# Adding expert results to a DRAM sum by whole rows, one add per block of tokens

## The chip, the cores and the metric

One core of one Trainium2 chip runs the kernel. The metric is the device time of one execution in microseconds (us); lower is better. Engines are called as in the profile: PE (TensorE, matrix products), PEld (its weight loads), DVE (VectorE), ACT (ScalarE), POOL (GpSimd), SP (SyncE, which here only issues DMAs).

## The reference

A decoder layer for one sequence of 1024 tokens of width 1024: two mixing branches, a projection, then a mixture of experts (MoE) that takes most of the time. What matters here is the MoE:

```python
top_val, top_idx = lax.top_k(logits, TOP_K)            # 4 of 32 experts a token
gate = jax.nn.softmax(top_val, axis=-1)
...
def expert_block(args):                                # a block of one expert's tokens
    xblk, e = args
    gu = xblk @ w_gu[e] + b_gu[e]                      # 1024 x 2048
    g, up = gu[:, :D_FF], gu[:, D_FF:]
    g = jnp.minimum(g, SWIGLU_LIMIT)
    up = jnp.clip(up, -SWIGLU_LIMIT, SWIGLU_LIMIT)
    act = (up + 1.0) * (g * jax.nn.sigmoid(SWIGLU_ALPHA * g))
    return act @ w_down[e] + b_down[e]                 # 1024 x 1024
...
out = jnp.zeros((N + 1, D_), f32).at[tok_buf].add(yb * w_buf[:, None])[:N]
```

Each token is in the list of four experts, so its output row is a sum of four expert results times their gates. A root-mean-square norm and a residual follow.

## The kernel before

Up to 570 us the kernel computes the mixing branches and the routing. From about 590 to 1980 us it runs the MoE. The experts are ordered by how many tokens they got, and each rank has a fixed capacity (`CAPS`, from 396 down to 36 token columns, 4648 in all). The 32 ranks go in eight groups of four (`GROUPS`), each of some 580 columns. For one group the kernel first does the gate and up products of all four experts, one half of the columns (c = 0, 1) after the other, then the down products, expert by expert, again in halves of 512 columns.

Weights come in chunks of 1 MiB on SP's queue (L1581) into six buffers `ST`. ACT makes a 16-bit high part of a chunk (L1585) and DVE the 16-bit rest (L1588), into seven buffers `WH`/`WL`; PE multiplies high by high and low activations (L1791, L1792) and rest by high ones (L1800). Twelve chunks make one expert's matrices, four of them the down matrix.

Results of a down product are scaled from PSUM into `yT`, transposed, in a region of 12.375 KB per partition; each half of an expert has its own piece, and a new piece waits for the transposes that read the piece it overwrites (L1839 to L1846). When one half of an expert is done, `out_jobs` (L1751) makes three jobs for each block of up to 128 tokens: four PE transposes into one of two PSUM banks `ot_` (L1759), an eviction by ACT or DVE that scales by the gate into one of three buffers `yt_r` of 128 x 512 (L1602 or L143 in the profile, tile A), and an indirect DMA on POOL (L1765) that adds the rows of 512 floats to one of two DRAM tensors `ff_d[c]`, at the rows that the token list names. Adds to the same `ff_d[c]` follow one another: each waits until the one before has landed. There are 51 blocks and so 102 adds. POOL's queue also issues the 51 gathers of token rows (L1726) for the next group.

The order on each engine is made beforehand: a planner (`Job`, `run_jobs`) goes through the jobs with estimated durations, due times and lags and writes each engine's instructions in the order in which it would start them. An add is planned with 1.7 us on POOL and 7.0 us more until it has landed. The engines then run their streams strictly in order; an instruction that waits holds up all behind it.

After the MoE, small loops for overflowing experts run zero times, and the sum is loaded from `ff_d` by eight DMAs (L1980) and normalised (L1988 and on); the results leave by SP.

Of the kernel before, what the change touches and what calls it, by code (L numbers as in the profile page):

```python
# [23 lines left out]
D = 1024  # L24
# [24 lines left out]
def hybrid_layer_kernel(ctx: ExitStack, tc: tile.TileContext, I, out):  # L49
# [777 lines left out]
    ff_d = [dr.tile([NR, D // 2], F32, name=f"ff_d{i}") for i in range(2)]  # L827
# [10 lines left out]
    for b in range(NR // 128):  # L838
        for q in range(2):
            P.dma_start(ff_d[q][128 * b:128 * b + 128], zt)  # L840
# [671 lines left out]

    SA = [slot(f"A{i}") for i in range(7)]
    ST = [carve(t_, 0, 4, 512) for t_ in SA[:-1]]
    WT.append(SA[-1])
    WH, WL = [], []
    for t_ in WT:
        WH.append(carve(t_, 0, 4, 256).bitcast(F16))
        WL.append(carve(t_, 4, 4, 256).bitcast(F16))
# [8 lines left out]
    X0, A0, Y0, XG0 = 0, XKB, 2 * XKB, 2 * XKB + 2 * CAPS[0] / 64  # L1528
    assert XG0 + 12 <= 64, XG0
# [6 lines left out]
    def acc_col():  # L1536
        n_acc[0] += 1
        return gacc[:, n_acc[0] - 1:n_acc[0]]
# [32 lines left out]
    def load_chunk(n):  # L1571
        if n >= len(chunks):
            i = n - len(chunks)
            if i < 4:
                SP.dma_start(HH[i], h_d[256 * i:256 * i + 256].rearrange("(b p) c -> p b c", p=128))
            else:
                SP.dma_start(GF, bass.AP(tensor=RW_d.tensor, offset=RW_d[1, 24].offset, ap=[[0, 128], [1, 1024]]))
        else:
            x, name, col, kh = chunks[n]
            load_expert(x)  # L1580
            SP.dma_start(ST[n % NST], I[name][0][ds(x.e, 1), 512 * kh:512 * kh + 512, col:col + 512]  # L1581
                         .rearrange("o (k p) c -> p (o k) c", p=128))
# [10 lines left out]
    n_mm, Y_KB = [0], 2 * CAPS[0] / 64  # L1593
# [76 lines left out]
    subs, phase = [], []  # L1670
    for gi, g in enumerate(GROUPS):
        phase.append((len(chunks), len(subs)))
        for c in range(2):
            for r in g:
                for q, kind in enumerate("gu"):
                    subs += [(kind, ex[r], c, js, len(chunks)) for js in (J4 if CAPS[r] <= 256 else J2)]
                    chunks += [(ex[r], "exp_w_gu", 1024 * q + 512 * c, kh) for kh in range(2)]
        phase.append((len(chunks), len(subs)))
        for r in g:
            for c in range(2):  # L1680
                subs += [("d", ex[r], c, js, len(chunks)) for js in (J4 if CAPS[r] <= 256 else J2)]
                chunks += [(ex[r], "exp_w_down", 512 * c, kh) for kh in range(2)]
    last_use, first_use = {}, {}
    for i, u in enumerate(subs):
        for kh in range(2):
            last_use[u[4] + kh] = i
            first_use.setdefault(u[4] + kh, 2 * i + kh)
# [61 lines left out]
    ot_free, yt_free, added, n_ot = [None] * 2, [None] * len(yt_r), [None] * 2, [0]  # L1749

    def out_jobs(x, c, b, yT, due, after):  # L1751
        cb = min(128, x.C - 128 * b)
        q, y = n_ot[0] % 2, n_ot[0] % len(yt_r)
        n_ot[0] += 1
        pt, yt = ot_[q], yt_r[y]

        def transpose(e):
            for k in range(4):
                PE.transpose(pt[0:cb, k], yT[:, k, 128 * b:128 * b + cb], ident)  # L1759
        t_ = Job({"PE": 0.46}, due, after + [ot_free[q]], transpose)  # L1760
        ot_free[q] = Job({"ACT": act_us(512, True), "DVE": dve_us(512)}, due + 2, [t_, yt_free[y]],
                         lambda e: scaled(e, yt[0:cb], pt[0:cb].rearrange("p a b -> p (a b)"),
                                          x.lt[0:cb, b, 1:2].bitcast(F32)))
# [11 lines left out]
    def sub_jobs(i, kind, x, c, js, n):  # L1775
        C, nj = x.C, len(js)
# [5 lines left out]
        us = nj * 4 * (max(C / 2400, 0.0225) + 0.0026)  # L1782
        needs = [bank_free[q] for q in bi] + (a_ready[x.r] if kind == "d" else x_ready[x.r])

        def highs(kh):
            def put(e):
                wh = WH[(n + kh) % NWS]
                for q, j in enumerate(js):
                    for k in range(4):
                        w_, f_ = wh[:, k, 128 * j:128 * j + 128], 4 * kh + k  # L1790
                        PE.matmul(pp[q], w_, mh[:, f_], start=(f_ == 0 and q % per == 0), stop=False, skip_group_check=True)  # L1791
                        PE.matmul(pp[q], w_, ml[:, f_], start=False, stop=False, skip_group_check=True)  # L1792
            return put

        def lows(kh):
            def put(e):
                wl = WL[(n + kh) % NWS]
                for q, j in enumerate(js):
                    for k in range(4):
                        PE.matmul(pp[q], wl[:, k, 128 * j:128 * j + 128], mh[:, 4 * kh + k], start=False,  # L1800
                                  stop=(kh == 1 and k == 3), skip_group_check=True)
            return put
        for kh in range(2):
            s_ = Job({"PE": 2 * us}, 2 * i + kh, [step[0], hi_[n + kh]] + (needs if kh == 0 else []), highs(kh))
            step[0] = Job({"PE": us}, 2 * i + kh, [s_, lo_[n + kh]], lows(kh))
            use[n + kh] = step[0]
        due, end = 2 * i + 4, step[0]
# [11 lines left out]
        elif kind == "u":  # L1819
            q, gs, gj = gs_of[x.r, js]  # L1820
            w = nj * C
# [5 lines left out]
            def clamp(e):  # L1827
                ts(u_t[:, 0:w], u_t[:, 0:w], 8.0, OP.min, -6.0, OP.max)
                stt(gs[:, 0:w], gs[:, 0:w], G_MAX, u_t[:, 0:w], OP.min, OP.mult)
            g3 = gs[:, 0:w].rearrange("p (j c) -> p j c", j=nj)  # L1830
            ev = Job({"ACT": act_us(w, True, nj), "DVE": dve_us(w, nj)}, due, [end, u_free[0]], linear)
            u_free[0] = Job({"DVE": dve_us(w, 2) + w / 1920}, due, [ev, gj], clamp)
            ah = Job({"ACT": act_us(w), "DVE": dve_us(w, 1, 1920)}, due + 2, [u_free[0]],
                     lambda e: scaled(e, x.ah[:, f0:f0 + nj], g3, XS))
            gs_free[q] = Job({"DVE": dve_us(w)}, due + 2, [ah],
                             lambda e: stt(x.al[:, f0:f0 + nj], g3, XS, x.ah[:, f0:f0 + nj], OP.mult, OP.subtract))
            a_ready.setdefault(x.r, []).append(gs_free[q])
        else:
            if js[0] == 0:  # L1839
                w = C / 64  # L1840
                at = y_at[0] if y_at[0] + w <= Y_KB else 0.0
                old = [o for o in y_used if o[0] < at + w and at < o[1]]
                for o in old:
                    y_used.remove(o)
                y_at[0] = at + w
                y_of[x.r] = (view(Y0 + at, 4, C), [t_ for o in old for t_ in o[2]], (at, at + w, []), [])  # L1846
            yT, wait, place, evs = y_of[x.r]

            def results(e):
                for k, j in enumerate(js):  # L1850
                    scaled(e, yT[:, j], pp[k], RS, x.bias[16 + f0 + k])
# [24 lines left out]
    for i, u in enumerate(subs):  # L1876
        while made < min(len(chunks) + 5, u[4] + 2):
            chunk_jobs(made)
            made += 1
        if i_ph % 2 and i_ph < len(phase) - 1 and phase[i_ph][1] == i:  # L1880
            todo = [(ex[r], b) for r in GROUPS[i_ph // 2 + 1] for b in range(NBS[r])]
            span_ = 2 * (phase[i_ph + 1][1] - i)
            for k, (x, b) in enumerate(todo):
                token_jobs(x, b, 2 * i + (span_ - 4) * k / len(todo), [ld[phase[i_ph - 1][0]], step[0]])
# [23 lines left out]
    zt = view(Y0, 512)  # L1908
    with tc.For_i(0, nzr, 1) as it:
        V.memset(zt, 0.0)  # L1910
        for q in range(2):
            SP.dma_start(ff_d[q][ds(it * 128, 128)], zt)
# [3 lines left out]
    def float_block(e, lt, bias):  # L1916
# [25 lines left out]
        for c in range(4):  # L1942
# [9 lines left out]
            if c % 2:  # L1952
                for k in range(4):
                    PE.transpose(ot_[0][:, k], yT[:, k], ident)
                scaled("ACT", yt_r[0], ot_[0].rearrange("p a b -> p (a b)"), lt[:, 0, 1:2].bitcast(F32))
                P.indirect_dma_start(out=ff_d[c // 2], in_=yt_r[0], in_offset=None, compute_op=OP.add,
                                     out_offset=bass.IndirectOffsetOnAxis(ap=lt[:, 0, 0:1], axis=0))
# [20 lines left out]
    for i in range(4):  # L1978
        for q in range(2):
            (SP, A)[q].dma_start(ft[i][:, :, 512 * q:512 * q + 512],  # L1980
                                 ff_d[q][256 * i:256 * i + 256].rearrange("(b p) c -> p b c", p=128))
# [37 lines left out]
```

## Time and profile before

| | us |
|---|---|
| median of 3 runs | 2026.05 (2025.1 to 2028.08) |
| profiled execution, its time | 2024.69 |
| profiled execution, its span | 2022.9 |
| mean granted clock of TensorE in it | 0.948 |

The time is that of an execution as the device gives it; the span is from the first to the last instruction in the trace, 1.8 us less. Busy times are of that one execution. A group's mean duration times its count gives busy time, not time on the path; what an engine waited for is read from the idle time ahead of an instruction. The granted clock is a share of 2.4 GHz: 1.00 is 2.4, 0.50 is 1.2.

### The profile page before, as it was taken

What the parts mean: (1) busy time and instruction counts of PE and PEld (TensorE: products, weight loads), DVE (VectorE), ACT (ScalarE), POOL (GpSimd) and SP (SyncE); (2) the same over time, 40 slices, a digit from 0 to 9 for tenths busy, and PEclk for the clock granted to TensorE, in tenths of its full rate; (3) what the DMA queues carried; (4) which work ended last, traced back from release to release, by engine and by line L of the source; (5) the groups of instructions that cost most, each with busy time, mean ns of one, the idle gap of its engine ahead of it and who ended that gap; (6) DMA issues with size and microseconds to landing.
All of it is one profiled execution on the core that took longest, in us unless ns stands there. A gap on an engine that the chain in (4) does not pass through costs nothing. (4 is left out here: it accounts for less than half of the span.)

```text
span 2022.9 us, 53263 instructions
## 1 busy us (share of the span) xinstructions
PE 1806.0 (89%) x22354; PEld 1614.5 (80%) x22354; DVE 1544.2 (76%) x2396; ACT 1199.1 (59%) x1682; POOL 526.5 (26%) x495
## 2 busy tenths in 40 slices
PE   8678699998968999998998899999899889999970
PEld 3566588787858999998998899767799789999870
DVE  5766537568767997995997799689799868869835
ACT  3524133544226876875776677577688667768641
POOL 4720012203543025015104402400330330160043
PEclk8889899999978999999999899999999989999985
DMA  9176465323359999999999899888999999999874
GB/s 310 39 193 132 137 196 161 126 70 131 115 172 326 363 322 353 379 351 307 323 329 358 278 351 341 279 323 301 299 367 365 301 296 330 327 318 350 306 192 175
DMA packets 296804, 540.82 MB, mean 267 GB/s; under 512 B 41234, under 2 KB 66032, under 8 KB 296528
## 3 DMA queue, kind: packets, MB, share of 16 engines
q1 hardware_dynamic: 259504, 469.51, 67.5%
q0 software_dynamic: 30384, 60.49, 11.8%
q10 hardware_dynamic: 6672, 7.38, 1.1%
q8 instruction: 177, 2.90, 0.6%
q14 instruction: 67, 0.55, 0.1%
HBM read 489.57 MB, written 45.61 MB: 265 GB/s over the span
## 5 line engine op out<-in xcount | busy, mean ns | idle before, releaser
L1765 POOL DMA_INDIRECT ff_d<-A,S x102 | 260.7, 2555 | 353.8 <-DVE A L143 141.2
L1588 DVE SCALAR_TENSOR_TENSOR B<-A,B 128x2048 f16<-128x2048 f32 x110 | 249.5, 2285 | 33.1 <-ACT B L1585 21.0
L1588 DVE SCALAR_TENSOR_TENSOR E<-A,E 128x2048 f16<-128x2048 f32 x110 | 249.7, 2285 | 16.0 <-ACT E L1585 15.8
L1726 POOL DMA_INDIRECT S<-hn_d,S x51 | 77.8, 1526 | 702.2 <-PE tr L1736 661.7
L1588 DVE SCALAR_TENSOR_TENSOR C<-A,C 128x2048 f16<-128x2048 f32 x110 | 249.7, 2284 | 8.3 <-ACT C L1585 8.2
L1585 ACT ACTIVATE B<-A 128x2048 f16<-128x2048 f32 x110 | 209.2, 1917 | 46.7 <-DMA A<-in_exp_w_gu_dram 36.7
L1585 ACT ACTIVATE E<-A 128x2048 f16<-128x2048 f32 x110 | 208.9, 1917 | 33.1 <-DMA A<-in_exp_w_gu_dram 18.4
L1585 ACT ACTIVATE C<-A 128x2048 f16<-128x2048 f32 x110 | 208.7, 1920 | 25.9 <-PE ax L1792 15.3
L1791 PE MATMUL mm<-S,E 128*128 128x92 f16 (+29 forms) x1336 | 187.8, 230 | 0.6 <-issue 0.5
L1791 PE MATMUL mm<-S,B 128*128 128x164 f16 (+28 forms) x1364 | 185.3, 227 | 3.3 <-issue 3.2
L1792 PE MATMUL mm<-S,B 128*128 128x164 f16 (+28 forms) x1364 | 184.9, 227 | 3.8 <-issue 3.8
L1792 PE MATMUL mm<-S,E 128*128 128x92 f16 (+29 forms) x1336 | 187.5, 229 | 0.0
L1792 PE MATMUL mm<-S,C 128*128 128x92 f16 (+28 forms) x1352 | 183.0, 226 | 3.2 <-issue 3.0
L1791 PE MATMUL mm<-S,C 128*128 128x92 f16 (+28 forms) x1352 | 183.2, 227 | 1.7 <-ACT S L1602 1.7
L1791 PEld LDWEIGHTS <-B 128*128 128x128 f16 x1760 | 154.3, 98 | 16.8 <-issue 9.4
L1791 PEld LDWEIGHTS <-C 128*128 128x128 f16 x1760 | 153.3, 98 | 13.0 <-issue 6.3
L1791 PEld LDWEIGHTS <-E 128*128 128x128 f16 x1760 | 155.0, 98 | 9.6 <-issue 2.0
L1792 PEld LDWEIGHTS <-B 128*128 128x128 f16 x1760 | 154.2, 98 | 9.4 <-issue 2.1
L1792 PEld LDWEIGHTS <-E 128*128 128x128 f16 x1760 | 154.9, 98 | 7.9 <-issue 0.4
L1792 PEld LDWEIGHTS <-C 128*128 128x128 f16 x1760 | 153.0, 98 | 8.3 <-issue 1.8
L148 DVE SCALAR_TENSOR_TENSOR S<-S 128x1 f32<-128x1 f32 (+7 forms) x249 | 106.0, 434 | 42.2 <-DMA S<-in_ada_w_dram 28.4
L1588 DVE SCALAR_TENSOR_TENSOR A<-A,A 128x2048 f16<-128x2048 f32 x54 | 123.5, 2286 | 3.1 <-ACT A L1585 2.9
(353 smaller groups left out, 4266.7 us busy)
## 6 DMA issues: line engine op xcount, KB each, us to landing
A<-in_exp_w_gu_dram SPq DMA_DIRECT2D x256, 1024.0 KB
A<-in_exp_w_down_dram SPq DMA_DIRECT2D x128, 1024.0 KB
S<-in_ada_w_dram POOLq DMA_DIRECT2D x64, 256.0 KB
S<-in_ada_w_dram SPq DMA_DIRECT2D x16, 512.0 KB
S<-in_w_in_dram SPq DMA_DIRECT2D x8, 1024.0 KB
S<-in_x_dram SPq DMA_DIRECT2D x12, 512.0 KB
ff_d<-S POOLq DMA_DIRECT2D x18, 256.0 KB
S<-in_w_out_dram SPq DMA_DIRECT2D x8, 512.0 KB
```

The costliest lines, as they stand in the source:

```text
L148: V.scalar_tensor_tensor(o, a, s, b, op0=op0, op1=op1, **kw)
L1585: A.activation(WH[n % NWS], ST[n % NST], AF.Copy, scale=WS)
L1588: V.scalar_tensor_tensor(WL[n % NWS], ST[n % NST], WS, WH[n % NWS], op0=OP.mult, op1=OP.subtract, accum_out=acc_col())
L1726: lambda e: P.indirect_dma_start(out=x_[0:cb], out_offset=None, in_=hn2_d, in_offset=bass.IndirectOffsetOnAxis(ap=x.lt[0:cb, b, 0:1], axis ...
L1765: lambda e: P.indirect_dma_start(out=ff_d[c], out_offset=bass.IndirectOffsetOnAxis(ap=x.lt[0:cb, b, 0:1], axis=0), in_=yt[0:cb], in_offset ...
L1791: PE.matmul(pp[q], w_, mh[:, f_], start=(f_ == 0 and q % per == 0), stop=False, skip_group_check=True)
L1792: PE.matmul(pp[q], w_, ml[:, f_], start=False, stop=False, skip_group_check=True)
```

## The change

The DRAM sum becomes one tensor of whole rows of 1024. The results of both halves of an expert stay in `yT` (a piece of twice the size, in a region of 20 KB instead of 12.375), and only when the second half is done do the jobs for its blocks follow: two times four transposes and two evictions into one of two buffers of 128 x 1024, then one add of whole rows. The add is planned with a lag of 9.0 us. Blocks of one expert are declared independent of one another; adds of different experts stay in order. A small POOL memset stands ahead of each add. The final load of the sum uses four DMAs of 1 MiB, one each for two blocks of tokens, instead of eight of 512 KiB.

Around it: the gather buffers move up in memory to make room, the column of accumulator results `gacc` shrinks to 256 columns and is summed once on the way, and chunks can have another width (`ROWS`), a possibility that is switched off by `ROWS = 0`, so that the weight chunks, products and their due times are as before. The core of the diff:

```diff
-    ff_d = [dr.tile([NR, D // 2], F32, name=f"ff_d{i}") for i in range(2)]
+    ff_d = dr.tile([NR, D], F32, name="ff_d")
...
+    ROWS = 0
...
-    yt_r = [carve(a7, 2 * i, 512) for i in range(3)]
-    gacc = carve(a7, 6, 500)
+    yt_r = [carve(a7, 4 * i, 1024) for i in range(2)]
+    gacc = carve(e3, 7, 256)
...
-    X0, A0, Y0, XG0 = 0, XKB, 2 * XKB, 2 * XKB + 2 * CAPS[0] / 64
+    Y_KB = 20
+    X0, A0, Y0, XG0 = 0, XKB, 2 * XKB, 2 * XKB + Y_KB
...
     def acc_col():
+        if n_acc[0] == 255:
+            V.tensor_reduce(gacc[:, 0:1], gacc, axis=AX.X, op=OP.add)
+            n_acc[0] = 0
...
-    def out_jobs(x, c, b, yT, due, after):
+    def out_jobs(x, b, yT, due, after, before, prev):
         cb = min(128, x.C - 128 * b)
-        q, y = n_ot[0] % 2, n_ot[0] % len(yt_r)
...
-        yt_free[y] = added[c] = Job({"POOL": 1.7}, due, [ot_free[q], added[c]],
-                                    lambda e: P.indirect_dma_start(
-                                        out=ff_d[c], out_offset=bass.IndirectOffsetOnAxis(ap=x.lt[0:cb, b, 0:1], axis=0),
-                                        in_=yt[0:cb], in_offset=None, compute_op=OP.add), lag=7.0)
-        return t_
+        y = n_ot[0] // 2 % len(yt_r)
+        yt, evs = yt_r[y], []
+        for c in range(2):
+            q = n_ot[0] % 2
+            n_ot[0] += 1
+            pt = ot_[q]
+
+            def transpose(e, pt=pt, c=c):
+                for k in range(4):
+                    PE.transpose(pt[0:cb, k], yT[:, 4 * c + k, 128 * b:128 * b + cb], ident)
+            t_ = Job({"PE": 0.46}, due, after + [ot_free[q]], transpose)
+            ot_free[q] = Job({"ACT": act_us(512, True), "DVE": dve_us(512)}, due + 2, [t_, yt_free[y]],
+                             lambda e, pt=pt, c=c: scaled(e, yt[0:cb, 512 * c:512 * c + 512],
+                                                          pt[0:cb].rearrange("p a b -> p (a b)"),
+                                                          x.lt[0:cb, b, 1:2].bitcast(F32)))
+            evs.append(ot_free[q])
+
+        def put(e):
+            P.memset(spacer, 0.0)
+            a_ = P.indirect_dma_start(out=ff_d, out_offset=bass.IndirectOffsetOnAxis(ap=x.lt[0:cb, b, 0:1], axis=0),
+                                      in_=yt[0:cb], in_offset=None, compute_op=OP.add)
+            for o_ in prev:
+                tc.declare_no_dep(a_.ins, o_.ins, reason="each token is in an expert's list once")
+            prev.append(a_)
+        yt_free[y] = Job({"POOL": 1.7}, due, evs + before, put, lag=9.0)
+        return t_, yt_free[y]
...
-            if js[-1] == 3:
-                place[2].extend(out_jobs(x, c, b, yT, due + 2, list(evs)) for b in range(x.NB))
+            if f0 + nj == 8:
+                prev, was = [], added[0]
+                for b in range(x.NB):
+                    t_, added[0] = out_jobs(x, b, yT, due + 2, list(evs), [was], prev)
+                    place[2].append(t_)
                 y_used.append(place)
...
     for i in range(4):
-        for q in range(2):
-            (SP, A)[q].dma_start(ft[i][:, :, 512 * q:512 * q + 512],
-                                 ff_d[q][256 * i:256 * i + 256].rearrange("(b p) c -> p b c", p=128))
+        (SP, A)[i % 2].dma_start(ft[i], ff_d[256 * i:256 * i + 256].rearrange("(b p) c -> p b c", p=128))
```

## Rows read from the trace of the kernel before

**Rows 1.** The page: the chain that ended last, by engine.
```profile
PE 28%; DMA 7%; issue 7%; DVE 2%; ACT 1%; DVEq 0%; ACTq 0%; POOL 0%; POOLq 0%
```

**Rows 2.** Windows: two stretches of adds, all seven's sum, one without, the whole.
```profile
core 0: us, PE busy (x) PEld busy (x) DVE busy (x) ACT busy (x) POOL busy (x), PEclk, DMA share, GB/s
...
1070.00:1162.00 92.00, 77.41 (x1214) 75.90 (x1213) 67.71 (x83) 58.77 (x72) 47.21 (x17) 0.93 0.95 315
...
1580.00:1666.00 86.00, 69.91 (x1114) 66.94 (x1113) 60.16 (x77) 52.89 (x64) 38.53 (x17) 0.92 0.99 292
...
sum 551.00, PE 506.79 PEld 474.51 DVE 417.87 ACT 364.14 POOL 267.82; mean PE 72.40 PEld 67.79 DVE 59.70 ACT 52.02 POOL 38.26
...
820.00:870.00 50.00, 50.00 (x790) 50.00 (x788) 49.31 (x51) 41.46 (x53) 0.00 (x0) 1.00 1.05 379
600.00:1928.00 1328.00, 1258.52 (x18745) 1170.69 (x18746) 1120.62 (x1423) 946.46 (x1149) 312.13 (x139) 0.97 0.97 329
```

**Rows 3.** Waits from 600 to 1945 us: who for whom, total us, times, longest.
```profile
ACT A L1602 <- DMA ff_d<-A,S: 81.1, 19, 13.0
POOL ff_d L1765 <- DMA ff_d<-A,S: 76.9, 19, 8.5
DVE A L143 <- DMA ff_d<-A,S: 26.8, 9, 8.1
PE ax L1759 <- DVE A L143: 18.5, 7, 6.1
...
PE ax L1759 <- ACT A L1602: 15.7, 3, 12.4
```

**Rows 4.** Windows: sum over five stretches of granted clock 0.50 at transposes' waits.
```profile
sum 27.20, PE 17.20 PEld 15.77 DVE 14.76 ACT 7.89 POOL 13.48; mean PE 3.44 PEld 3.15 DVE 2.95 ACT 1.58 POOL 2.70
```

**Rows 5.** The chain in order of time: start, us, what; amid the MoE and at its end.
```profile
1119.96 19.36 DMA ff_d<-A,S x2
...
1939.67 14.05 DMA ff_d<-A,S
...
1954.81 6.97 DMA ff_d<-A,S
...
1983.66 5.22 DMA S<-ff_d
```

**Rows 6.** DMA queues (packets, MB, share): 779 to 815 us, then 880 to 903.
```profile
q1 hardware_dynamic: 5628, 11.18, 83.8%
q0 software_dynamic: 880, 1.34, 20.5%
...
q0 software_dynamic: 560, 0.95, 11.5%
```

**Rows 7.** Timeline of POOL: routing scatters with a memset ahead, then gathers.
```profile
580.57 0.11 POOL L1408 MEMSET S<- 128x1 f32 x1
580.86 0.96 POOL L1409 DMA_INDIRECT L_d<-S  x1 [0.19 <-issue]
...
582.13 0.96 POOL L1409 DMA_INDIRECT L_d<-S  x1 [0.19 <-issue]
...
589.57 1.14 POOL L1726 DMA_INDIRECT S<-hn_d,S  x1 [0.31 <-issue]
601.35 0.92 POOL L1726 DMA_INDIRECT S<-hn_d,S  x1 [10.63 <-DVE S L1498]
```

**Rows 8.** All adds by their line: duration ns min/median/max, first and last start.
```profile
L1765 POOL DMA_INDIRECT ff_d<-A,S x102: 1330/1977/15047, 744.7 to 1977.4; - x102
```

**Rows 9.** Timelines at the end: PE, DVE and POOL.
```profile
1958.43 0.55 PE L1800 MATMUL mm<-S,E 128*128 128x36 f16 x16
...
1958.06 0.67 DVE L1894 TENSOR_REDUCE S<-A 128x1 f32<-128x500 f32 x1
...
1977.43 1.40 POOL L1765 DMA_INDIRECT ff_d<-A,S  x1 [1.29 <-DMA ff_d<-A,S]
1988.95 3.38 POOL L133 TENSOR_TENSOR S<-S,A 128x1024 f32<-128x1024 f32 x1 [10.12 <-DMA S<-ff_d]
1993.03 11.57 POOL L133 TENSOR_TENSOR S<-S,A 128x1024 f32<-128x1024 f32 x5 [0.70 <-DMA S<-ff_d]
```

More of the change, by code (lines that the diff above doesn't have):

```diff
@@ L1578, in load_chunk @@
         else:
[L1579 removed]
+            x, name, col, kh, w = chunks[n]
             load_expert(x)
[L1581 to L1582 removed]
+            nr = 128 * 2048 // w
+            SP.dma_start(ST[n % NST].rearrange("p (k c) -> p k c", c=w),
+                         I[name][0][ds(x.e, 1), nr * kh:nr * kh + nr, col:col + w].rearrange("o (k p) c -> p (o k) c", p=128))
     def split_hi(n):
@@ L1667, in run_jobs, with sub_units @@
         return max(free.values())
-    subs, phase = [], []
+    subs, phase, n_step = [], [], [0]
+    def sub_units(kind, r, c, turn):
+        whole = CAPS[r] <= ROWS
+        name, col = {"g": ("exp_w_gu", 0), "u": ("exp_w_gu", 1024), "d": ("exp_w_down", 0)}[kind]
+        if whole:
+            if c != turn:
+                return
+            c = 0
+        nk = 4 if whole else 2
+        for js in ([tuple(range(8))] if whole else J4 if CAPS[r] <= 256 else J2):
+            subs.append((kind, ex[r], c, js, len(chunks), nk, n_step[0]))
+            n_step[0] += nk
+        chunks.extend((ex[r], name, col + 512 * c, kh, 1024 if whole else 512) for kh in range(nk))
     for gi, g in enumerate(GROUPS):
         phase.append((len(chunks), len(subs)))
+        some = [r for r in g if CAPS[r] <= ROWS]
         for c in range(2):
             for r in g:
-                for q, kind in enumerate("gu"):
-                    subs += [(kind, ex[r], c, js, len(chunks)) for js in (J4 if CAPS[r] <= 256 else J2)]
-                    chunks += [(ex[r], "exp_w_gu", 1024 * q + 512 * c, kh) for kh in range(2)]
+                for kind in "gu":
+                    sub_units(kind, r, c, int(r in some[-(len(some) // 2):]))
         phase.append((len(chunks), len(subs)))
@@ L1680, in hybrid_layer_kernel @@
             for c in range(2):
[L1681 to L1687, printed above, removed]
+                sub_units("d", r, c, 0)
+    first_use = {}
+    for u in subs:
+        for kh in range(u[5]):
+            first_use.setdefault(u[4] + kh, u[6] + kh)
     ld, hi_, lo_, use = {}, {}, {}, {}
@@ L1746, in token_jobs @@
             xg_free[slot_] = t_
-    ot_free, yt_free, added, n_ot = [None] * 2, [None] * len(yt_r), [None] * 2, [0]
-    def out_jobs(x, c, b, yT, due, after):
+    ot_free, yt_free, added, n_ot, adds = [None] * 2, [None] * len(yt_r), [None], [0], []
+    def out_jobs(x, b, yT, due, after, before, prev):
         cb = min(128, x.C - 128 * b)
-        q, y = n_ot[0] % 2, n_ot[0] % len(yt_r)
[L1754 to L1763, printed above, removed]
-        yt_free[y] = added[c] = Job({"POOL": 1.7}, due, [ot_free[q], added[c]],
-                                    lambda e: P.indirect_dma_start(
-                                        out=ff_d[c], out_offset=bass.IndirectOffsetOnAxis(ap=x.lt[0:cb, b, 0:1], axis=0),
-                                        in_=yt[0:cb], in_offset=None, compute_op=OP.add), lag=7.0)
-        return t_
@@ L1876, in hybrid_layer_kernel @@
     for i, u in enumerate(subs):
-        while made < min(len(chunks) + 5, u[4] + 2):
+        while made < min(len(chunks) + 5, u[4] + u[5]):
             chunk_jobs(made)
```

88 lines of the change are left out of this document (44 added, 44 removed).

## The prediction, made before the changed kernel ran

> **What bounds the kernel now.** I read the chain first, then the stages, then the waits. The chain that ended last is PE for 28% of the span and DMA for 7% [rows 1]; the DMA in it is nearly all adds to `ff_d`. By stages, PE is busy 1258.5 of the 1328 us from 600 to 1928 [rows 2], so the MoE runs at PE's pace with some 70 us of holes. DMA engines come close behind: their share is 0.97 there. But packets overlap, and a stretch without adds shows what the queue can do: 379 GB/s against a mean of 329 [rows 2]. 1328 x 329 / 379 = 1153 us would carry the same bytes, so DMA has about 13% in hand and PE about 5%.
>
> Where are the holes? Seven stretches, in which the first seven groups add their results, last 551 us, and PE is idle in 44 of them, 14.6 and 16.1 in the two worst, those with an expert of three blocks [rows 2]. The waits name the cause as a chain of three: ACT waits 81.1 us (19 times) and DVE 26.8 us (9 times) for an add to land, since the eviction needs its `yt` buffer; PE's transposes then wait for the bank that ACT or DVE should have emptied, 15.7 + 18.5 = 34.2 us in 10 waits [rows 3]. POOL itself waits 76.9 us for the add before. Only PE's 34.2 us are time of the kernel; the others mostly stand beside running products. In the chain two adds in a row take 19.36 us, 9.7 each from issue to landing; single ones there take 7 to 14 [rows 5].
>
> After some of these waits the granted clock reads 0.50, 1.2 GHz instead of 2.4. In the five such stretches PE is busy for 17.2 us [rows 4], work that full clock would do in half: 8.6 us.
>
> **The change, part by part.**
>
> *The chain of adds, in the groups.* Ninety half-row adds in seven groups, 12.9 a group, stand in stretches of 79 us on average (551 / 7). In one half's chain some 6.4 blocks follow one another: 6.4 x 9.7 = 62 us, nearly the whole stretch, so any late landing reaches PE. After it, four experts a group follow one another, and the 2.4 further blocks cost only POOL's issue, 1.98 us median [rows 8]. What a whole-row add takes is not in the trace. Its data: in a stretch with adds and no gathers, queue 0 moved 1.34 MB, some 654 packets of 2 KB, in 20.5% of 16 engines for 36 us, 118 us or 0.18 us a packet; a weight packet of 2 KB there took 0.838 x 576 / 5459 = 0.088, and a gather's packet of 4 KB 0.115 x 368 / 232 = 0.18 [rows 6]. Adding 2 KB thus costs as much as moving 4, and 4 KB should cost between 0.27 (one more read of 0.09 beside the gather's 0.18) and 0.36. With 128 rows on 16 engines an add grows by 8 x 0.09 to 8 x 0.18, 0.7 to 1.4 us, or by 8 x (0.18 + 0.09) = 2.2 where a row goes as two packets with a weight packet between: 9.7 becomes 10.4 to 11.9. I take 11.5, near the dearer end, since weights are nearly always loading. Chain per group: 4 x 11.5 + 2.4 x 2.0 = 51 us of 79. It no longer fills the stretch, and an expert's adds have landed before the next expert's results come.
>
> What stays: two buffers hold two blocks, where three held one and a half. The third and later blocks of the ranks with 396, 272 and 260 columns still wait for a landing. I keep one mean wait (3.4 us) for each of the three: 10 us of 34.2 stay, **24 us go**, and with them the same share of the clock's loss, 8.6 x 24 / 34.2 = **6 us**. Bounds: nothing goes, or all 34.2 + 8.6 = 43. Late next, where a transpose no longer waits, is the weights' high part: PE's holes are then 45 us of 1298, and DMA would have to carry 337 GB/s of 379. I expect that to hold.
>
> *The end.* The last product ends at 1959.0, the last add starts at 1977.4, and the load of the sum is issued at 1983.7 [rows 5, 9]: 25 us of adds behind one another. In the new order the last group has only three experts' adds left at about 1950. Results of the last large expert (two blocks) are free of the ACT stall that ends at 1953.7 with an add of 14.05 us [rows 5], so its first add can start at some 1956, an estimate. Such an add took 6.97 us here, weights being done [rows 5]; with 1.4 us for its data it lands at 1964.4, its second, 2 us behind, at 1966.4. The last expert (36 rows) adds behind it. From its add's start to the load it is 1983.66 - 1977.43 = 6.2 us now, landing and loop ends together [rows 5, 9]; so the load goes out at 1972.7 instead of 1983.7, **11 us**. Bounds: 5, if the two blocks still follow one another, to 14.
>
> *The final load.* The first piece came 5.22 us after issue [rows 5]. Now two pieces of 1 MiB share the engines at first, so the first is whole only when two are: POOL's products, which start at 1988.95 and have one gap of 0.70 [rows 9], start some 3.5 us later and run without it. They are in one row to the end. **Costs 3 us**; bounds 0 and 4.
>
> *Small things, with one answer.* 51 memsets of 0.11 us with 0.19 of idle [rows 7] on POOL, ahead of the gathers in its queue, against 51 issues of 1.98 us less: POOL is busy 312 of 1328 us [rows 2], nothing; without that cover 15 us. The one reduction of 256 columns is under the 0.67 us of the one over 500 [rows 9]. The second gather buffer now lies over the overflow table's scratch, so the second gather, at 589.57, would go when the third does, at 601.35, behind those tables [rows 7]. Its landing still falls near the transposes that use it; 0, at most 3 us. Transposes and evictions are as many as before, but come in pairs after an expert instead of half by half; PE has other products between them. 0 to 26 us of DMA time (9296 packets of 0.18 against 4648 of 0.27 to 0.36, over 16 engines) is off the path.
>
> **Sum**: 2024.7 - 24 - 6 - 11 + 3 = 1986.7 for the profiled execution. The median is 1.4 above it: 1988.
>
> **Rivals.**
>
> *Weights become the bound.* DMA share 0.97 to 0.99 in the worst stretches [rows 2] speaks for it, the 379 GB/s against it. PE's 30 us come back as waits for weights, and only the end is won: 2024.7 - 8 = 2017, median 2018. A packet of an add would take the engine for up to four weight packets, and the rate while adds run is lower already (292 and 315 against 379, [rows 2]). The Trainium skill (DMA: Bandwidth & Descriptors, Queues, rings and completion order) says that an engine takes turns between queue rows packet by packet; by that, weights get one turn per longer packet and wait longer at a time. The rates of these rows agree in direction; by that rule the time would be this rival's 2018, if the buffers of 13 chunks ran dry.
>
> *The order stays.* If a wait on the last add remains in spite of the declaration, 6.4 blocks x 11.5 = 74 us a group fill the stretch as before, and the end wins 5 less 3: median 2024. Against it: the routing scatters are built in the same way, and start 1.27 us after one another [rows 7], far under any landing.
>
> *Slower: buffers are held too long.* A whole-row buffer is taken from the first eviction to the landing of twice the bytes. If landing time goes with the bytes (9.7 to 19 us), four experts and their blocks need more than the 79 us of a stretch; it decides from about 18 us. The 28 waits for a landing then last twice as long, and PE's part with them: + 34, the clock + 9, the end as now, the load + 3: 2024.7 + 46 = 2071, median 2072. Against it: an add's 128 packets are only 1.4 us of its 9.7.
>
> *More is won.* All 34 + 9 go, and ACT, no longer held 81 us, brings the weights' parts earlier, so that half of PE's other holes in these stretches goes (44 - 34 = 10, so 5) and 8 elsewhere: 2024.7 - 43 - 13 - 11 + 3 = 1961, median 1962.
>
> **How the numbers follow.** Forecast 1988 with 0.48; more won 0.13; weights 0.16; order stays 0.10; slower 0.13. From 1960 to 2023 lie the first three cases and a little of the fourth, some 0.79. A measurement of this kernel can tell about 0.2% (4 us) from no change. Faster: 0.48 + 0.13 + most of 0.16 + a little of the fourth = 0.79; same 0.09; slower 0.12.
>
> **What would show it.** Right: 51 adds, those of one expert 2 to 4 us apart, none waiting for its own expert's; waits of ACT and DVE for `ff_d` down from 108 to some 40 us, of the transposes from 34 to 10; the final load issued about 14 us after the last product instead of 25. If transposes' waits shrink but waits for weights (L1791, L1792 after L1585) grow by as much, the second case holds. If adds take 18 us or more, or PE's holes in the stretches exceed 44 us, the forecast is wrong at its chain; if the first piece of the sum lands within 6 us of issue, the load's cost is wrong.

## The result, and the profile after

The change made the kernel slower by half a per cent: median 2035.88 us (14 runs, 2032.01 to 2040.13) against 2027.09 us for the kernel before. Two of the kernel before's 14 runs were slow ones, 2286.87 and 3646.74 us, and the ratio leaves them out. The ratio of the times is 1.0052, with a 95% interval from 1.0038 to 1.0066. The forecast was 1988 us, with a range from 1960 to 2023: the time lies outside it, on the other side of no change. The profiled execution took 2036.72 us (span 2034.8, mean granted clock 0.943, before 0.948).

The adds first: all of them by their line (count, duration on POOL in ns as min/median/max, first and last start, and in the last row us from start to landing).

```profile
L1791 POOL DMA_INDIRECT ff_d<-A,S x51: 1349/2233/16201, 749.6 to 1985.2; - x51
...
DMA to landing us min/median/max: 4.1/9.4/29.2
```

Half as many adds as in [rows 8]. Their median landing is under the 11.5 us of the prediction: 9.4 us for the 25 adds whose landing this view gives, and 9.7 us for all 51 by the increments of their semaphores, of which more below. But the maximum is 29.2 us, on which no step of the prediction counted. Next the waits, over the stretch of [rows 3] (who for whom, total us, times, longest).

```profile
POOL ff_d L1791 <- DMA ff_d<-A,S: 70.5, 7, 16.2
...
DVE A L143 <- DMA ff_d<-A,S: 61.2, 8, 14.9
...
ACT A L1608 <- DMA ff_d<-A,S: 39.3, 7, 14.1
...
PE ax L1781 <- ACT A L1608: 36.4, 5, 12.8
...
PE ax L1781 <- DVE A L143: 1.7, 1, 1.7
```

These are the rows that answer to [rows 3]. ACT and DVE still wait for landings, 39.3 + 61.2 = 100.5 us against 107.9. PE's waits at the output transposes are 36.4 + 1.7 = 38.1 us in 6 where they were 34.2 in 10: fewer, and longer. PE's busy time shows the same in the whole stretch of [rows 2]: 1249.31 of 1328 us, 9 less than before.

```profile
600.00:1928.00 1328.00, 1249.31 (x18657) 1163.14 (x18658) 1114.62 (x1402) 943.19 (x1152) 207.13 (x139) 0.97 0.97 327
```

Which adds are late? They come in a fixed order, so each one's block, and with it the number of rows, is known from the capacities (204 columns are blocks of 128 and 76). Here are single adds, each in a window of its own: the second block of 204 columns (76 rows), the block of 92, the third block of 260 (4 rows), and one of 120 for comparison.

```profile
L1791 POOL DMA_INDIRECT ff_d<-A,S x1: 3842/3842/3842, 760.1 to 760.1; - x1
DMA to landing us min/median/max: 15.5/15.5/15.5
...
L1791 POOL DMA_INDIRECT ff_d<-A,S x1: 16201/16201/16201, 1106.9 to 1106.9; - x1
DMA to landing us min/median/max: 29.2/29.2/29.2
...
L1791 POOL DMA_INDIRECT ff_d<-A,S x1: 2672/2672/2672, 1617.3 to 1617.3; - x1
DMA to landing us min/median/max: 16.9/16.9/16.9
...
L1791 POOL DMA_INDIRECT ff_d<-A,S x1: 1622/1622/1622, 1297.8 to 1297.8; - x1
DMA to landing us min/median/max: 6.4/6.4/6.4
```

76, 92 and 4 rows land late, 120 rows early: neither the bytes nor the number of rows orders them. What the late ones share is their largest divisor up to 16, which is 4. Seven of the 51 blocks are so (76, 116, 92, 4, 92, 124 and 68 rows). Measured from the end of the issue they land after 13.2 us on average, and the groups with divisors from 10 to 16 after 5.9 to 7.8 us. In the kernel before, the same seven blocks' half-row adds land some 7.6 us behind their issue and the others 5.9, so half rows had hidden most of the difference.

The trace shows more of a landing: each add raises its semaphore sixteen times, and the last increment is the landing. Times are us from the end of the issue:

| add at | rows | largest divisor up to 16 | increments |
|---|---|---|---|
| 1937.09 | 128 | 16 | 16 at 6.7 to 8.2 |
| 1977.04 | 100 | 10 | 6 at 2.0 to 2.4, 10 at 5.1 to 5.7 |
| 1106.93 | 92 | 4 | 12 at 5.9 to 6.1, 4 at 12.9 to 13.0 |
| 1942.97 | 124 | 4 | 12 at 6.3 to 7.8, 4 at 16.0 to 17.1 |
| 1964.36 | 68 | 4 | 12 at 1.1 to 1.2, 4 at 7.4 to 7.9 |

So the data of a late add ends in four places, as many as its divisor, and the other twelve are done early. PE's long stalls at the transposes (6.4, 12.8, 11.5 and, at the end, 8.7 us) stand behind one of the seven each; one of 4.3 us, in the group with the expert of four blocks, doesn't.

The end is the second place. The timeline of POOL (start, duration, in brackets the idle time before and what ended it):

```profile
1937.09 2.89 POOL L1791 DMA_INDIRECT ff_d<-A,S  x1 [116.33 <-ACT A L1608]
...
1942.97 3.38 POOL L1791 DMA_INDIRECT ff_d<-A,S  x1 [2.87 <-issue]
...
1964.36 1.76 POOL L1791 DMA_INDIRECT ff_d<-A,S  x1 [17.89 <-issue]
...
1974.81 1.57 POOL L1791 DMA_INDIRECT ff_d<-A,S  x1 [8.58 <-DMA ff_d<-A,S]
...
1985.21 1.42 POOL L1791 DMA_INDIRECT ff_d<-A,S  x1 [6.45 <-DMA ff_d<-A,S]
```

The add at 1942.97 has 124 rows. It lands at 1963.5, after 20.5 us, and the next expert's add, which is ordered behind it, starts only then. That one has 68 rows and lands 9.7 us later. The load of the sum goes out at 1992.4, 29.4 us after the last product at 1963.0; before it was 24.7 us, at 1983.66 [rows 5]. Its first piece then takes, by the chain of work that ended last (start, us, what):

```profile
1992.43 8.44 DMA S<-ff_d
```

That is 3.2 us more than the 5.22 of [rows 5].

Two legs sum this up, taken from starts and ends in the traces: from the first gather to the last product, and from there to the end of the span. What lies ahead of the first gather, 583 to 591 us, scatters between runs of kernels that are the same up to there.

| kernel | first gather to last product, us | last product to end, us |
|---|---|---|
| before | 1370.8 | 63.9 |
| after | 1377.4 | 71.8 |
| after, adds rounded to 16 rows | 1352.0 | 61.3 |
| after, gathers rounded | 1356.3 | 73.5 |
| after, both rounded | 1342.3 | 60.2 |
| after, three buffers | 1342.0 | 71.2 |
| after, both rounded, three buffers | 1328.1 | 59.4 |
| before, both rounded | 1355.7 | 58.2 |

So the change lost 6.6 us in the groups and 7.9 at the end. The other kernels are those of the experiments.

### The profile page after: what moved, and what is told of

Its sections match the earlier page's. It is cut to its first block, busy times and chain, and to the rows that moved or that the text cites. A ratio compares the mean times of both kernels' runs of the same rounds, so it can differ in the third digit from the quotient of the medians.

```text
span 2034.8 us, 53189 instructions
## 1 busy us (share of the span) xinstructions
PE 1804.4 (89%) x22354; PEld 1613.9 (79%) x22354; DVE 1546.4 (76%) x2399; ACT 1198.0 (59%) x1680; POOL 413.2 (20%) x495
## 5 line engine op out<-in xcount | busy, mean ns | idle before, releaser
L1594 DVE SCALAR_TENSOR_TENSOR C<-A,C 128x2048 f16<-128x2048 f32 x110 | 250.1, 2287 | 25.7 <-ACT C L1591 25.7
L1594 DVE SCALAR_TENSOR_TENSOR E<-A,E 128x2048 f16<-128x2048 f32 x110 | 249.9, 2287 | 19.6 <-ACT E L1591 19.5
L1594 DVE SCALAR_TENSOR_TENSOR B<-A,B 128x2048 f16<-128x2048 f32 x110 | 249.9, 2287 | 12.0 <-ACT B L1591 11.7
L1745 POOL DMA_INDIRECT S<-hn_d,S x51 | 77.1, 1511 | 752.2 <-PE tr L1755 683.5
L1791 POOL DMA_INDIRECT ff_d<-A,S x51 | 142.0, 2784 | 427.5 <-ACT A L1608 205.5
L1591 ACT ACTIVATE C<-A 128x2048 f16<-128x2048 f32 x110 | 208.8, 1918 | 23.8 <-DMA A<-in_exp_w_gu_dram 15.8
L1821 PEld LDWEIGHTS <-C 128*128 128x128 f16 x1760 | 153.5, 98 | 10.4 <-issue 3.3
L1594 DVE SCALAR_TENSOR_TENSOR A<-A,A 128x2048 f16<-128x2048 f32 x54 | 123.5, 2287 | 5.8 <-ACT A L1591 5.7
## 6 DMA issues: line engine op xcount, KB each, us to landing
A<-in_exp_w_gu_dram SPq DMA_DIRECT2D x256, 1024.0 KB, 10.4
```

The costliest lines, as they stand in the source:

```text
L1591: A.activation(WH[n % NWS], ST[n % NST], AF.Copy, scale=WS)
L1594: V.scalar_tensor_tensor(WL[n % NWS], ST[n % NST], WS, WH[n % NWS], op0=OP.mult, op1=OP.subtract, accum_out=acc_col())
L1745: lambda e: P.indirect_dma_start(out=x_[0:cb], out_offset=None, in_=hn2_d, in_offset=bass.IndirectOffsetOnAxis(ap=x.lt[0:cb, b, 0:1], axis ...
L1791: a_ = P.indirect_dma_start(out=ff_d, out_offset=bass.IndirectOffsetOnAxis(ap=x.lt[0:cb, b, 0:1], axis=0), in_=yt[0:cb], in_offset=None, c ...
```

## Experiments

Each time below is given as a ratio to the kernel before, measured on the same chip in the same hour; one per cent is 20.3 us. The kernel after stands at +0.52%. A difference between two of these ratios carries the intervals of both, about half a point (10 us) either way for most pairs.

| kernel | ratio | interval | median us |
|---|---|---|---|
| after, adds rounded to 16 rows | 0.9896 | 0.9843 to 0.9950 | 2004.87 |
| after, gathers rounded | 0.9982 | 0.9958 to 1.0005 | 2019.26 |
| after, both rounded | 0.9812 | 0.9771 to 0.9854 | 1988.22 |
| after, three buffers | 0.9886 | 0.9859 to 0.9913 | 2005.72 |
| after, both rounded, three buffers | 0.9742 | 0.9717 to 0.9766 | 1975.50 |
| after, both rounded, load by half rows | 0.9836 | 0.9812 to 0.9860 | 1993.33 |
| after, seven more blocks made bad | 1.0088 | 1.0065 to 1.0111 | 2040.51 |
| after, ordered | 1.0130 | 1.0081 to 1.0179 | 2051.47 |
| after, both rounded, ordered | 0.9888 | 0.9852 to 0.9923 | 2000.94 |
| after, ring of before | 1.0071 | 1.0043 to 1.0098 | 2038.47 |
| before, adds rounded | 0.9951 | 0.9930 to 0.9973 | 2015.96 |
| before, both rounded | 0.9876 | 0.9841 to 0.9912 | 1999.33 |

**Rounded rows in the adds.** The buffer's further rows hold old values, and the token list sends them to dummy rows.

```diff
-            a_ = P.indirect_dma_start(out=ff_d, out_offset=bass.IndirectOffsetOnAxis(ap=x.lt[0:cb, b, 0:1], axis=0),
-                                      in_=yt[0:cb], in_offset=None, compute_op=OP.add)
+            cp = min(128, -(-cb // 16) * 16)
+            a_ = P.indirect_dma_start(out=ff_d, out_offset=bass.IndirectOffsetOnAxis(ap=x.lt[0:cp, b, 0:1], axis=0),
+                                      in_=yt[0:cp], in_offset=None, compute_op=OP.add)
```

> The kernel after, with the rows of every add rounded up to a multiple of 16; the rows beyond the block hold old values and are added to the 128 dummy rows behind the tokens, since no expert holds more tokens than its list length here. Theory A (the row count): an add whose rows divide by 4 and by nothing more up to 16 (76, 116, 92, 4, 92, 124 and 68 rows, 7 of the 51) lands late because its rows are shared by 4 DMA engines; their mean landing behind the end of the issue, 13.2 us, falls to the 7 us of the others, most of the 41 us of PE's waits at the output transposes go with them and the tail gets 8 to 10 us shorter: 1990 to 2008 us. Rival B (the buffers): a whole-row add under the weight loads holds one of two buffers for about 10 us whatever its row count, and the late adds are late for what they run beside: the time stays at 2030 to 2040 us and the seven landings stay above 11 us.

0.9896, 1.56 points or some 32 us under the kernel after, though more rows are moved. The seven landings behind the issue fell from 13.2 to 8.0 us on average. The 124 rows of the end, now 128, and those of the block of 4 rows, now 16:

```profile
L1793 POOL DMA_INDIRECT ff_d<-A,S x1: 2877/2877/2877, 1924.3 to 1924.3; - x1
DMA to landing us min/median/max: 10.9/10.9/10.9
...
L1793 POOL DMA_INDIRECT ff_d<-A,S x1: 2201/2201/2201, 1596.8 to 1596.8; - x1
DMA to landing us min/median/max: 16.9/16.9/16.9
```

20.5 us became 10.9. One add stayed at 16.9. Ahead of it on POOL stand gathers with row counts of the same kind (the first of these two has 124 rows, the second 68), here in the timeline:

```profile
1592.01 2.51 POOL L1746 DMA_INDIRECT S<-hn_d,S  x1 [0.30 <-issue]
1594.82 1.68 POOL L1746 DMA_INDIRECT S<-hn_d,S  x1 [0.31 <-issue]
...
1596.81 2.20 POOL L1793 DMA_INDIRECT ff_d<-A,S  x1 [0.19 <-issue]
```

And their line over this stretch. The maximum is that of the 68 rows; the view gives no landing for the 124 rows, whose semaphore is full 20.0 us after the start:

```profile
DMA to landing us min/median/max: 8.2/13.4/18.6
```

The waits of PE at the transposes (stretch of [rows 3]) are more than halved, 17.0 us against 38.1, and the longest, 8.5 us, stands behind this add:

```profile
PE ax L1782 <- ACT A L1609: 16.6, 5, 8.5
...
PE ax L1782 <- DVE A L143: 0.4, 1, 0.4
```

**Rounded rows in the gathers too**, by the same edit at L1745.

> The kernel after, with the rows of the adds and of the gathers rounded up to a multiple of 16. In the run with rounded adds alone the longest wait left at the output transposes, 8.65 us at 1606 us, stood behind an add of 16 rows that landed 16.9 us after its start, beside gathers of 124 and 68 rows that took 17.5 and 16.9 us behind their issue. Theory A (the gathers' row counts hold the same few DMA engines): that add lands in 8 to 10 us, the gathers of 76, 116, 92, 124, 68 and 92 rows fall from 8 to 17 us to 5 to 9 us, and the time is 6 to 14 us under that of rounded adds alone: 1990 to 1999 us. Rival (that add is late for the weights, or for another reason in that stretch): no difference, 2001 to 2009 us, the add at 16 us still.

0.9812, another 0.84 points (17 us; the intervals overlap a little, from 0.9843 to 0.9854). The add of 16 rows landed in 10.4 us, the seven blocks in 7.0 us behind their issue, and PE's longest wait at the transposes fell from 8.5 to 5.8 us:

```profile
PE ax L1783 <- ACT A L1609: 14.7, 5, 5.8
...
PE ax L1783 <- DVE A L143: 1.3, 2, 0.9
```

In the profiled runs 9.7 us of the lead over rounded adds alone lie between the first gather and the last product, within theory A's 6 to 14; 7.5 us are there before the first gather, and are scatter. The 17 us of the ratios are a little over that range.

**The gathers alone.**

> The kernel after, with the rows of the gathers alone rounded up to a multiple of 16. Theory A (the adds' own row counts make most of the late landings; the gathers make the one of 4 rows at 1617 us and slow weight pieces): the 4-row add lands in under 12 us, the other six stay late, and the time is 5 to 18 us under the kernel after, 2018 to 2031 us. Rival (gathers matter only when the adds are in time): 2031 to 2040 us.

0.9982, 0.70 points (14 us) under the kernel after, all of it ahead of the last product (1356.3 us against 1377.4). The six other adds land as they did in the kernel after (29.3 us for the 92 rows at 1102), and the one of 4 rows is not late any more, with its 4 rows:

```profile
L1792 POOL DMA_INDIRECT ff_d<-A,S x1: 1426/1426/1426, 1599.4 to 1599.4; - x1
DMA to landing us min/median/max: 10.9/10.9/10.9
```

So this one was late for the gathers in front of it, and not for its own count. In the kernel after its increments come in three parts, 8 at 7.1 to 7.5 us, 4 at 11.1 to 11.5 and 4 at 13.8 to 14.2; here all 16 come at 6.7 to 9.5.

**The reverse: seven good blocks made bad.**

```diff
+            cp = {112: 116, 120: 124, 64: 68, 88: 92, 108: 116, 60: 68}.get(cb, cb)
```

> The kernel after, with rows added (at most 8, to dummy rows) to the adds of 112, 120, 64, 88, 108 and 60 rows, seven blocks in all, so that they too divide by 4 and by nothing more up to 16 (116, 124, 68, 92, 116, 68). Theory A: these seven land in 13 us behind their issue where they took 5 to 8, and the time rises by 8 to 30 us, to 2044 to 2066 us. Rival B (what counts is the bytes and the load beside them): at most 8% more rows, 2031 to 2041 us, and their landings stay near 7 us.

All seven landed late, 11 to 17 us behind their issue instead of 5 to 9. Here are two of them, both 120 rows made 124; the first is the block that landed in 6.4 us above, the second took 11.4 us in the kernel after.

```profile
L1794 POOL DMA_INDIRECT ff_d<-A,S x1: 2242/2242/2242, 1298.8 to 1298.8; - x1
DMA to landing us min/median/max: 17.8/17.8/17.8
...
L1794 POOL DMA_INDIRECT ff_d<-A,S x1: 2706/2706/2706, 1771.7 to 1771.7; - x1
DMA to landing us min/median/max: 19.4/19.4/19.4
```

Four more rows on 120 cost 8 to 11 us: it is the count and not the bytes. The Trainium skill (DMA: Bandwidth & Descriptors, Why a DMA increments its semaphore by 16 and not by 1) gives a rule for it: a transfer is spread over as many engines as the largest number up to 16 that divides the slowest dimension of both its sides. By that, 124 rows go to 4 engines, 31 each, and 128 to 16, 8 each. The runs with rounded rows and this one agree with it, and so do the increments, twelve early and four late; which engines they are, the trace doesn't tell. The kernel's time rose less than expected, to 1.0088, 0.36 points (7 us) over the kernel after, just under theory A's 8 us and over the 5 us of rival B; the intervals touch at 1.0065. Three of the seven are the last block of their group, with no add behind them for some 100 us: a late landing can cost time only where a buffer or the next expert's add is wanted before it. Where the 7 us lie isn't shown: in the profiled execution (2035.49 us, among the fastest of its ten) PE's waits at the transposes are 36.6 us, no more than in the kernel after.

**A third buffer, no rounding.**

```diff
-    Y_KB = 20
+    Y_KB = 16
...
+    yt_r.append(view(XG0 + 12, 1024))
```

> The kernel after, with three whole-row result buffers in place of two (the ring of expert results gives 4 of its 20 KB for the third). Rival B (two buffers are too few for a landing of 10 us): the waits of ACT and DVE for an add's landing, 56 us and 76 us, fall below a third, and the time to 1990 to 2010 us, as with the rounded rows. Theory A (seven adds and the gathers beside them are late for their row counts; a third buffer covers one late add but not the load of four DMA engines behind it, nor the order between experts): half of the 41 us of PE's waits go, the tail keeps its 20 us landing: 2012 to 2028 us.

0.9886, as much as the rounded adds bring, although six of the seven adds stay late (the 124 rows still 20.6 us; the one of 4 rows now lands in 7.3, and the 60 rows, which now stand behind the gathers of 124 and 68 rows, in 15.7). The evictions wait a third as long for them, 33.3 us in the stretch of [rows 3] where it was 100.5, and PE 10.6 us at the transposes (the third buffer is called S):

```profile
DVE A L143 <- DMA ff_d<-A,S: 11.1, 2, 7.0
ACT S L1609 <- DMA ff_d<-S: 10.4, 2, 7.6
...
DVE S L143 <- DMA ff_d<-S: 9.8, 2, 7.1
...
PE ax L1782 <- DVE A L143: 6.2, 2, 4.5
...
PE ax L1782 <- ACT A L1609: 4.4, 2, 4.2
...
ACT A L1609 <- DMA ff_d<-A,S: 2.0, 1, 2.0
```

Rival B's figures came, and theory A's for this run were too pessimistic. Read with the rounded runs, it takes both for a stall: an add that lands late, and no free buffer behind it. Either cure removes most of it. Not so at the end, where there is no cure in a buffer: the later experts' adds are ordered behind the late one. From the last product to the end it takes 71.2 us here as in the kernel after (71.8), and 61.3 with rounded adds.

**Both cures.**

> Rounded adds and gathers, and three result buffers. If, with the rounded rows, two buffers no longer hold the work up, the third brings 0 to 5 us over the same kernel with two: 1988 to 1998 us. If buffers were a limit of their own beside the row counts, 8 us or more: 1975 to 1987 us.

0.9742, the fastest of all, 2.6% under the kernel before, and 0.70 points (14 us) under the same with two buffers: so two buffers are a limit of their own, if a smaller one. PE is busy 1280.34 of 1328 us in the stretch of [rows 2], the granted clock over the span is 0.956, and the queue carries 335 GB/s:

```profile
600.00:1928.00 1328.00, 1280.34 (x19256) 1192.43 (x19256) 1140.34 (x1446) 965.06 (x1179) 217.97 (x151) 0.98 0.97 335
```

**Without the declaration.**

```diff
-            for o_ in prev:
-                tc.declare_no_dep(a_.ins, o_.ins, reason="each token is in an expert's list once")
```

> The kernel after, without the declaration that the blocks of one expert do not depend on each other: each whole-row add waits for the landing of the one before. Prediction's account: the declaration is worth the chain of adds within an expert, so the time rises by 15 to 35 us, to 2050 to 2070 us. Rival (two buffers bind already, so that the order adds nothing): 2031 to 2041 us.

1.0130, 0.78 points (16 us) slower than the kernel after, at the low end of the prediction's account. The same with rounded rows:

> The kernel after with rounded adds and gathers, but each add waits for the landing of the one before, within an expert too (no declaration). Among the unrounded kernels the declaration was worth 15.6 us (2051.5 against 2035.9). If it is worth that through the chain of landings itself, here too 10 to 18 us: 1998 to 2006 us. If it only took late adds off each other's backs: under 5 us, 1986 to 1993 us.

0.9888, 0.76 points (15 us) over the rounded kernel with the declaration. The two intervals just meet (0.9852 and 0.9854), so 15 us is the likely value and not a sharp one. As far as that goes, its worth does not hang on the late adds: it is that of landings that follow one another.

**The kernel before, rounded.** First its adds alone:

> The kernel before, with the rows of every add (half rows, in order) rounded up to a multiple of 16 in the same way. Theory A: the waits of before at the output transposes, 37 us, stand behind the same seven blocks, so they shrink here too, though less (half the bytes on the four engines): 2008 to 2018 us. Rival B (the chain of ordered adds binds in before, whatever the row count): 2022 to 2030 us.

0.9951, 10 us, which is within theory A's range. But PE's waits at the transposes, which by theory A would shrink, did not (34.8 us against 34.2), so only a little of its account holds here. Then adds and gathers:

> The kernel before (half rows, every add in order, three half-row buffers) with the rows of its adds and gathers rounded up to a multiple of 16. It tells what the change itself is worth once no row count is a bad one: its time against the 1988 us of the change with the same rounding. Prediction's account (the order and the smaller pieces cost the kernel before some 36 us, whatever the row counts): 2008 to 2016 us, so that the change is worth 20 us or more. Rival (the order cost time only through the few late adds): 1986 to 1998 us, and the change is worth nothing by itself.

0.9876: 25 us from the rounding, between the two accounts. PE's waits in the stretch of [rows 3] are now 14.4 + 11.9 = 26.3 us:

```profile
PE ax L1762 <- ACT A L1604: 14.4, 4, 8.9
...
PE ax L1762 <- DVE A L143: 11.9, 4, 4.4
```

The rounded kernel after stands 0.64 points (13 us) under it; the intervals overlap at their ends (0.9841 and 0.9854), so 13 us is the likely value and not a sharp one. The legs agree: 13.4 us less up to the last product, 2.0 more behind it.

**The ring of results.**

> The kernel after, with the ring of expert results at the 12.4 KB of before in place of 20 KB. Two buffers that wait for late adds hold back the output transposes and with them the ring: if the larger ring gives room there, 5 to 20 us more than the kernel after, 2041 to 2056 us. Rival (the output transposes stand in PE's order anyway, so the ring never fills): 2031 to 2040 us.

1.0071 against 1.0052, intervals overlapping: no difference that can be told. The larger ring is room for the new order, and no cost or gain of it shows.

**The final load in eight pieces.**

> Rounded adds and gathers, and the final load in eight pieces of half rows, 256 tokens each, as in the kernel before, in place of four pieces of whole rows. Prediction's account (the first 128 tokens are there 3 us later with whole-row pieces): 2 to 5 us less than the same kernel with four pieces, 1987 to 1995 us. Rival (the load as a whole sets the end, its pieces do not): within 1.5 us of it.

```diff
-        (SP, A)[i % 2].dma_start(ft[i], ff_d[256 * i:256 * i + 256].rearrange("(b p) c -> p b c", p=128))
+        for c in range(2):
+            (SP, A)[i % 2].dma_start(ft[i][:, :, 512 * c:512 * c + 512],
...
```

0.9836 against 0.9812: no gain, but the run doesn't decide between the two accounts, because its pieces don't go as in the kernel before. There the two halves of a row went at the same time, one on SP and one on ACT; here both go on the same queue, one behind the other, and the other queue's first piece belongs to the next 256 tokens. By their semaphores the first two pieces landed 3.8 and 5.0 us after the first issue, as early as in the kernel before (4.6 and 5.2). But the second half of the first tokens landed only after 9.0 us, and the products start right behind it:

```profile
1943.73 2.45 SPq L2015 DMA_DIRECT2D S<-ff_d  x4
...
1952.80 1.23 DVE L133 TENSOR_TENSOR S<-S,A 128x1024 f32<-128x1024 f32 x1 [18.17 <-DMA S<-ff_d]
```

With four pieces and both roundings SP's first piece, whole rows, landed after 6.56 us:

```profile
1944.99 6.56 DMA S<-ff_d
```

Halves on two queues, as before, weren't tried with whole rows in the sum.

## Why the prediction was wrong

*What bounds the kernel.* The mechanism was read rightly: an add lands, an eviction waits for its buffer, a transpose waits for its bank. What was missed stood in the same rows: waits of 13.0 us beside means of 4 and 3 us [rows 3], and in the chain 9.71 us for one add of 128 rows and 14.05 [rows 5] for another, 11 us later:

```profile
1928.79 9.71 DMA ff_d<-A,S
```

Such a spread calls for a cause of its own before a mean is taken.

*The chain of adds in the groups, −24 and −6.* This is the step that failed. It spread every add over 16 engines ("128 rows on 16 engines", 8 packets each), priced it at 11.5 us and asked whether a group's chain of 51 us fits its 79. The median came lower, 9.4 us; but the time goes to the few adds of 15 to 29 us, whose increments show four engines at work. There a whole row puts twice the data on the same few engines while it holds one of only two buffers. The price of a packet was not the fault: an estimate with the prediction's 0.27 to 0.36 us gives 31 packets on each of four engines 8.4 to 11.2 us, and the last four increments of the 124 rows come 9.6 us behind the other twelve on average. PE's waits went from 34.2 to 38.1 us, not to 10, and the granted clock went down from 0.948 to 0.943 instead of up. With rounded rows the term can be measured: PE's waits are 26.3 us in the kernel before and 16.0 in the kernel after, 10 us less, and the leg up to the last product is 13.4 us shorter. That is a little under half of the 30 us put down for waits and clock.

*The declaration.* This held. The adds at 1974.8 and 1977.0, both of the expert with 228 columns, are 2.2 us apart, and the two runs without it are 15 and 16 us slower. The rival in which the order stays is out.

*Whole rows by themselves.* The sum of the runs' ratios says what the prediction's parts were worth. Without rounding: whole rows in two buffers, ordered, +1.30%, 26 us slower; the declaration −0.78, 16 us; together the +0.52% of the result. With rounded rows: ordered whole rows +0.12 (0.9888 against 0.9876), no difference that can be told; the declaration −0.76, 15 us. So the loss is one of whole rows with bad counts; of whole rows by themselves none shows.

*The end, −11.* This failed. The load was to go out 14 us after the last product, and went 29.4 us after it: the 124 rows take 20.5 us, and the later experts' adds are ordered behind them. The estimate let the last large expert's first add start at 1956; it started at 1974.81. Its price was not the fault: 8.4 us were put down for the landing, taken from 6.97 us for a half-row add of 68 rows, one of the bad counts, and it took 6.3. Without the bad counts the load goes out 19.7 us after the last product (rounded, two buffers), but 18.7 us in the rounded kernel before, so there was nothing to win here either. The likely reason, which no run isolates: half rows were being added while the last products ran, and whole rows have to wait for the second half.

*The final load, +3.* It measured 3.2 us. The cause given, two pieces of 1 MiB that share the engines at first, fits the traces of the same load: the first piece takes 8.4 and 9.1 us where the two are issued 0.07 us apart (the kernel after, with and without the declaration), 6.2 to 7.9 us where they are 0.09 to 0.22 us apart, and 4.96 us in the one trace where they are 0.45 us apart (both rounded, three buffers):

```profile
1935.36 4.96 DMA S<-ff_d
```

No run was made for that, so it is argued and not shown.

*Small things.* Nothing in the runs speaks against their 0. POOL's busy time in the stretch of [rows 2] fell from 312 to 207 us, and nothing followed from that.

*Rivals.* "Buffers are held too long" was the right direction and the right place; its price was tied to the bytes, deciding at 18 us for all adds, where it is the row count, for seven of them. "Weights become the bound" is out: the fastest kernel moves 335 GB/s in the stretch in which the kernel before moved 329 [rows 2], and PE is busy 22 us more. That the rounded kernel takes 1988 us, the figure of the forecast, is chance: 25 us of its way there are rounding that the kernel before can have too.

## What to carry to other kernels

Before an indirect DMA is made larger, look at the divisors of its row counts: a count whose largest divisor up to 16 is 4 landed 4 to 11 us later than the same block with another count, and held up what queued behind it; rounding the count up cost nothing to speak of, since dummy rows could take the rest (the other blocks' landings stayed at 7.0 us behind their issue, from 7.1). Where a ring of buffers waits on landings, count the buffers against the longest landing in the trace and not against the median. Price a chain by its late links.

## What the runs showed of the hardware

The long issue on POOL was not expected. The add of 92 rows at 1106.93 kept POOL for 16.2 us where the median is 2.2, in the kernel after, and 15.8 us with rounded rows. DVE's timeline beside it has no gap: up to 1121.3, 1.8 us before the issue ends, seven splits of weights (L1594, two inputs from SBUF) follow one another, with one eviction of 0.75 us among them.

```profile
1106.93 16.20 POOL L1791 DMA_INDIRECT ff_d<-A,S  x1 [7.38 <-DMA ff_d<-A,S]
...
1107.29 2.29 DVE L1594 SCALAR_TENSOR_TENSOR A<-A,A 128x2048 f16<-128x2048 f32 x1
...
1119.01 2.29 DVE L1594 SCALAR_TENSOR_TENSOR E<-A,E 128x2048 f16<-128x2048 f32 x1
```

The other issues of over 5 us in the traces of before, after and four of the experiments (adds rounded, both rounded, three buffers, and both), 22 of them, run beside back-to-back splits in the same way. Splits cover 81% of the issues over 5 us on average, and 23% of those under 2 us in the same traces. With three buffers and rounded rows the same add's issue took 2.4 us, and it landed in 9.0. The Trainium skill (SBUF — State Buffer, SBUF: two separate sides) tells of a port pair that GpSimd and VectorE share, and that an instruction of VectorE with two SBUF inputs holds for its whole length against a GpSimd operation that reads SBUF. The overlap agrees with that if the issue of an indirect DMA is such an operation, which the page doesn't say. No run took the splits away, so the cause stays argued and not shown.
